# First FFN: meta products of gate and up in one group, a pair's differences put off, the first gate's sums in the opening

## The chip, the cores and the metric

The kernel runs on one core of a Trainium2 chip. Its engines are TensorE (PE, with the weight loads shown apart as PEld), VectorE (DVE), ScalarE (ACT), GpSimd (POOL) and SyncE (SP, whose queue issues most transfers); each works through its own instructions in order. The metric is the device time of one execution in microseconds.

## The reference

One layer of a hybrid decoder for 1024 tokens and 16 learned meta tokens, in float32, with model width 1024 and a feed-forward width of 2816:

```python
def swiglu(h, w_in, w_out):
    gu = h @ w_in
    g, u = jnp.split(gu, 2, axis=-1)
    return (jax.nn.silu(g) * u) @ w_out

# h = h + 1/2 * swiglu(rms_norm(h))         first feed-forward layer (FFN)
# u = rms_norm(h) @ w_in                    projection
# o = concat[hgrn2(u), stick_breaking(u)]   parallel heads
# h = h + o @ w_out
# h = h + 1/2 * swiglu(rms_norm(h))         second FFN
```

The change touches the first FFN, and in one place the second product of both FFNs.

## The kernel before

**Numbers in two halves.** A float32 operand is split into a high half in fp32r (a cast on ACT, L360, `wh`) and the rest (a subtraction on DVE, L362, `wl`). A product is the sum of high by high, low by high and high by low (`times`, L430). Four blocks of 128 in the contracted dimension make 12 matmuls of 128x128 by 128x512 for one product.

**Seven products for eight.** `fast_in` computes x @ w_in for a block of 256 columns of the weights, as a 2x2 of blocks by the 2x2 of the tokens and model halves, with seven products in place of eight. One such block is a quad. Its order on TensorE is: B11 (bank qa), T2 (qb), B21 (qa), T3 (qb), the meta tokens' small products, T1 (qc), T4 (qb), B22 (qc). Their weights are a11, s2, a12, s3, s1, a22 and s4 in this order: three raw blocks, and four sums made on POOL (L384): s1 = a21 + a22, s2 = s1 - a11, s3 = a11 - a21, s4 = a12 - s2. Between products DVE or ACT read the bank: `p1` after B11, u2 = p1 + qb after T2 (L462, `kept`), u3 after T3. T3 adds into the same bank as T2, so it may start only when DVE has read u2. In the same way B21 adds into qa after p1 was read. `take` reads the four output banks (L504 to L507 for the gate, L513 to L517 for the up quad).

**Pairs.** A gate quad and the up quad of the same 256 columns are a pair; there are 11 (f = 0, 2 ... 20). `up` multiplies silu(gate) by up into `sg`, and after the last of the four quarters `combined` makes four differences of them on DVE (L533 twice, L540, L543), which the second product needs as operands; POOL stores each of them (L529, L520). The first four pairs, the openers, run with gate and up in turns. Their first two products stand in the opening, in which tokens are transposed, scaled and halved into TensorE's operands (`open_tokens`; L829 to L831 for the differences that T2 and T3 are made of, L892 for T4's).

**Meta tokens.** The 16 meta tokens go through the same weights with 32-column matmuls (`meta_in`): `begin` does 16 of them per quad in the tile `mq` (32 records in the trace, four at a time on quarters of the array, L937); ACT copies the result (`mt`, L947), and `finish`, called by the next group, adds the pieces up with a matmul by `pick` (`mf`, L917) followed by Silu or the product with it. The meta group is the last reader of a quad's raw blocks, so the next quad's loads (L373, on SP) wait for it: `in_bufs` raw buffers, six.

**What sets the order.** TensorE's order in the first FFN is the order in which the code is written. In `open_tokens` that of ACT, DVE and SP is too. Elsewhere a scheduler orders ACT, DVE, POOL and SP; `issue_after` adds an edge to it. `between` (one step of a list of work for later stages at 54 `hooks`) splits the weights of the projection and the second FFN ahead of time: an early load on SP (L152), a cast on ACT (L174), a subtraction on DVE (L175) and a store on SP (L169), in `both` tiles.

**Second product.** `fast_out` multiplies the stored activations by w_out in the same way (products L685, weights and operands split in L617 and L618). It evicts a finished set of four banks into `hT` with four DVE operations (L657), for most steps delayed to the second quarter of the next step.

## Time and profile before

| What | us |
| --- | --- |
| median of three runs | 2023.78 |
| lowest and highest | 2022.3, 2026.27 |
| profiled execution, device time | 2020.56 |
| its span in the trace | 2018.8 |

The device time of the profiled execution is 1.8 us longer than its span. Times in the trace count from the span's start, and L12 is line 12 of the program. In the rows of a timeline stand start, duration, engine, line, operation, output and inputs by the program's names, the tile's shape and how many were put together; in brackets, how long the engine was idle ahead of it and what it waited for. In tables of waits stand the engine and line that waited, what they waited for, and then the total in us, how many times, and the longest. The stages of the span are: start to 16, opening to 100, opener pairs to 203, single pairs to 490, the first FFN's second product to about 700, then projection, mixing and the second FFN from 1380 to the end.

### The profile page before, as it was taken

The numbers are of one execution on the slowest core, as the hardware profiler recorded it, in microseconds if no ns is written. First come the engines' busy times: TensorE is split into PE (matmuls) and PEld (weight loads), VectorE is DVE, ScalarE is ACT, GpSimd is POOL, SyncE is SP. The second block draws the span as 40 slices with busy tenths as digits, with TensorE's granted clock in tenths as the row PEclk, the third lists the DMA queues.
The fourth block names the chain that finished last, engine by engine and source line by source line (L and its number), as shares of the span: only waits on it lengthen the run. The fifth ranks groups of instructions, "written<-read, shape, count | busy, mean of one in ns | idle before, by whom it ended". The sixth has DMA issues, their size and how long they took to land.

```text
span 2018.8 us, 30806 instructions
## 1 busy us (share of the span) xinstructions
PE 1964.1 (97%) x10940; PEld 1646.2 (82%) x10940; DVE 1356.4 (67%) x2052; ACT 860.8 (43%) x1742; POOL 583.5 (29%) x692
## 2 busy tenths in 40 slices
PE   7999999999999999999999999999999999999998
PEld 6788777777878888888888888777888888888887
DVE  7867667787578663237767667558566766767764
ACT  6423333333444544456666635434132333344443
POOL 3443233332000002334333341320444545530000
PEclk9999999999999999999999999999999999999999
DMA  6266787757985416343545166664533233369363
GB/s 206 83 171 182 227 260 245 241 185 255 327 278 164 131 53 204 123 169 101 139 133 139 55 229 179 167 238 162 194 102 110 101 103 103 106 253 310 116 198 136
DMA packets 315578, 347.19 MB, mean 172 GB/s; under 512 B 61520, under 2 KB 216656, under 8 KB 315424
## 3 DMA queue, kind: packets, MB, share of 16 engines
q1 hardware_dynamic: 297136, 292.18, 46.0%
q0 software_dynamic: 17248, 53.03, 7.5%
q8 instruction: 87, 1.43, 0.3%
q14 instruction: 67, 0.55, 0.1%
q10 hardware_dynamic: 1040, 0.00, 0.0%
HBM read 233.75 MB, written 111.38 MB: 171 GB/s over the span
## 4 chain that ended last, share of the span: by engine, by line
PE 82%; DVE 7%; DMA 5%; issue 3%; ACT 2%; POOL 1%; SPq 0%; DVEq 0%; POOLq 0%; ACTq 0%
PE o L685 18%; PE qb L430 16%; PE qc L430 11%; PE qa L430 10%; PE proj L249 5%; PE proj L251 5%; PE proj L250 5%; PE flip L1366 2%; DMA raw<-in_ffn_w_out_dram 1%; PE wo L250 1%; PE wo L249 1%; PE wo L251 1%; PE mq L937 1%; PE oacc L1436 1%; PE oacc L1438 1%
## 5 line engine op out<-in xcount | busy, mean ns | idle before, releaser
L430 PE MATMUL qb<-T,wh 128*128 128x512 f32 x1056 | 346.0, 391 | 10.1 <-DVE u L462 7.5
L430 PEld LDWEIGHTS qb<-T,wh 128*128 128x128 f32 x1056 | 198.1, 188 | 58.4 <-ACT both L174 5.7
L430 PE MATMUL qa<-B,wh 128*128 128x512 f32 x696 | 227.0, 390 | 2.2 <-DVE sum L513 1.9
L362 DVE TENSOR_TENSOR wl<-s,wh 128x512 fp32r<-128x512 f32 x160 | 183.4, 1147 | 60.4 <-ACT wh L360 59.3
L249 PE MATMUL proj<-xh,wh 128*128 128x512 f32 (+2 forms) x640 | 216.5, 338 | 0.8 <-DVE st L1059 0.7
L685 PE MATMUL o<-t,w 128*128 128x512 f32 x924 | 213.1, 391 | 1.3 <-DVE w L618 1.1
L251 PE MATMUL proj<-xl,wh 128*128 128x512 f32 (+2 forms) x640 | 209.7, 328 | 0.8 <-DVE xl L1821 0.8
L250 PE MATMUL proj<-xh,wl 128*128 128x512 f32 (+2 forms) x640 | 209.9, 328 | 0.0
L685 PE MATMUL o<-parts 128*128 128x512 f32 x924 | 209.9, 389 | 0.0
L430 PE MATMUL qb<-T,wl 128*128 128x512 f32 x528 | 206.0, 390 | 1.5 <-DVE wl L362 1.4
L685 PEld LDWEIGHTS o<-t,w 128*128 128x128 f32 x924 | 172.6, 188 | 39.0 <-DVE w L618 1.5
L685 PEld LDWEIGHTS o<-parts 128*128 128x128 f32 x924 | 173.4, 188 | 36.0
L360 ACT CAST wh<-s 128x512 fp32r<-128x512 f32 x160 | 99.4, 622 | 227.1 <-PE qb L430 168.3
L430 PEld LDWEIGHTS qa<-B,wh 128*128 128x128 f32 x696 | 130.5, 188 | 30.3 <-ACT T L309 2.3
L384 POOL TENSOR_TENSOR s<-raw 128x512 f32<-128x512 f32 x80 | 109.8, 1372 | 153.6 <-DMA raw<-in_ffn_w_in_dram 89.3
L430 PE MATMUL qa<-B,wl 128*128 128x512 f32 x348 | 135.5, 389 | 0.0
L360 ACT CAST wh<-raw 128x512 fp32r<-128x512 f32 x120 | 74.5, 621 | 142.6 <-PE qc L430 103.7
L251 PEld LDWEIGHTS proj<-xl,wh 128*128 128x128 f32 x640 | 120.5, 188 | 12.3 <-DVE xl L1821 1.2
L249 PEld LDWEIGHTS proj<-xh,wh 128*128 128x128 f32 x640 | 120.7, 189 | 11.4 <-DVE st L1059 1.2
L250 PEld LDWEIGHTS proj<-xh,wl 128*128 128x128 f32 x640 | 120.6, 188 | 9.1
L1518 POOL TENSOR_TENSOR sig<-sig,keep 128x144 f32<-128x144 f32 (+3 forms) x64 | 81.4, 1273 | 133.7 <-DVE keep L1512 94.1
L430 PE MATMUL qc<-T,wh 128*128 128x512 f32 x352 | 118.6, 398 | 0.0
(392 smaller groups left out, 4023.2 us busy)
## 6 DMA issues: line engine op xcount, KB each, us to landing
raw<-in_ffn_w_in_dram SPq DMA_DIRECT2D x176, 256.0 KB, 3.5
raw<-in_ffn_w_out_dram SPq DMA_DIRECT2D x121, 256.0 KB, 4.4
w2in<-both SPq DMA_DIRECT2D x28, 512.0 KB, 2.9
raw<-in_w_in_dram SPq DMA_DIRECT2D x25, 512.0 KB, 4.1
ks<-kD SPq DMA_DIRECT2D x32, 260.0 KB, 4.8
wout<-both SPq DMA_DIRECT2D x16, 512.0 KB, 3.8
wh<-w2in SPq DMA_DIRECT2D x27, 256.0 KB, 3.2
wl<-w2in SPq DMA_DIRECT2D x27, 256.0 KB, 3.2
```

The costliest lines, as they stand in the source:

```text
L249: nc.tensor.matmul(ps, wh[:, s], xs, start=k == 0, stop=False)
L250: nc.tensor.matmul(ps, wl[:, s], xs, start=False, stop=False)
L251: nc.tensor.matmul(ps, wh[:, s], xl[:, k, c0 : c0 + n], start=False, stop=k == nk - 1)
L360: nc.scalar.copy(hi, src)
L362: nc.vector.tensor_sub(lo, src, hi.bitcast(F32))
L384: taken(op(t, x, y), False)
L430: nc.tensor.matmul(ps, a[:, k, :], b[:, k, :], start=start and k == 0 and i == 0, stop=k == 3 and i == 2, skip_group_check=True,)
L685: nc.tensor.matmul(banks[bank][m], y[:, m * P : (m + 1) * P], z, start=start and at == 0 and e == 0, stop=q == nq - 1 and e == 2, skip_gro ...
L937: nc.tensor.matmul(ps[at : at + 32, :], self.xm[:, 4 * h + k, :], blocks[i, h][:, k, :], start=h == 0 and kk == 0, stop=h == 1 and kk == 1 ...
L1366: self.nc.tensor.transpose(ps[:m, j, :], src[:, s0 : s0 + m], self.ident)
L1436: nc.tensor.matmul(o[:, c], vj, w[0], start=j == 0, stop=False, skip_group_check=True)
L1518: nc.gpsimd.tensor_mul(sig, sig, keep[:, 1 : nk + 1])
```

## The change

Seven edits, by place:

- Meta products (`meta_in`): the gate's blocks are kept, and gate and up are multiplied in one group of 32 matmuls (64 records) in the up quad, ahead of its T1; one copy of `mt` and two `mf` matmuls in a row. There are 11 groups instead of 22. `in_bufs` goes from 6 to 10.
- `put_off`: `combined` of a pair in the first FFN is called in the next gate quad, after its u3, that is, after its T3 is written out.
- `prepare`: the first gate's four blocks are loaded and its four sums made on POOL at the opening's item 4. Their buffers and the early loads' are divided differently (early loads 8 to 4; raw blocks of the opening come from the common pool).
- The opening: T2's differences are made with T2's and T3's halves, those of T4 only behind the last tokens' work; T4's and B22's halves come a step later each.
- `split_ahead`: a plain group is one piece, and a load goes ahead only where both groups fit in four buffers. The list has 58 steps instead of 54 and still 54 hooks; what is left over is done at the start of the second product (three `both` copies).
- `fast_out`: a delayed eviction of four banks is done in two halves, two banks in the second quarter and two in the fourth.
- A filler tile is 32 instead of 288 columns.

```diff
-                t = self.early_raw.tile([P, 512], F32, tag="raw", name="early", bufs=8)
+                t = self.early_raw.tile([P, 512], F32, tag="raw", name="early", bufs=4)
...
-            nxt = load(groups[0][0])
-            yield None
-            for (_, makes), after in zip(groups, groups[1:] + [((), None)]):
-                raws, nxt = nxt, load(after[0])
+            ahead = []
+            for i, (views, makes) in enumerate(groups):
+                if not ahead:
+                    ahead.append(load(views))
+                    yield None
+                raws = ahead.pop(0)
+                after = groups[i + 1 : i + 2]
+                if after and len(views) + len(after[0][0]) <= 4:
+                    ahead.append(load(after[0][0]))
...
-        return [
-            ([v for _, v in pieces[i : i + 4]],
-             [(d, lambda raws, j=j: raws[j]) for j, (d, _) in enumerate(pieces[i : i + 4])])
-            for i in range(0, len(pieces), 4)
-        ]
+        return [([v], [(d, lambda raws: raws[0])]) for d, v in pieces]
...
-        loaded = []
-
-        def block(i, h, col, turns=0):
-            if turns == 2:
-                t = self.early_raw.tile([P, 4, P], F32, tag="raw", name="raw", bufs=self.ahead_bufs)
-            else:
-                t = wp.tile([P, 4, P], F32, tag="raw", name="raw", bufs=self.in_bufs)
...
+        prepared = {}
+        quarters = (0, 0), (1, 0), (1, 1), (0, 1)
+
+        def first_sums(blocks, turns):
+            a11, a21, a22, _ = blocks
+            s1 = made(a21, nc.gpsimd.tensor_add, a22, turns)
+            return s1, made(s1, nc.gpsimd.tensor_sub, a11, turns)
+
+        def prepare(col):
+            blocks = [block(i, h, col) for i, h in quarters]
+            a11, a21, _, a12 = blocks
+            s1, s2 = first_sums(blocks, 2)
+            s3 = made(a11, nc.gpsimd.tensor_sub, a21, 2)
+            prepared[col] = blocks, (s1, s2, s3, made(a12, nc.gpsimd.tensor_sub, s2, 2))
...
-            blocks = [block(i, h, col, turns) for i, h in quarters]
+            blocks, sums = prepared.pop(col, (None, None))
+            blocks = blocks or [block(i, h, col) for i, h in quarters]
             a11, a21, a22, a12 = blocks
             if not opened:
                 yield operand(a11)
-            s1 = made(a21, nc.gpsimd.tensor_add, a22, turns)
-            s2 = made(s1, nc.gpsimd.tensor_sub, a11, turns)
+            if sums:
+                s1, s2, s3, s4 = sums
+            else:
+                s1, s2 = first_sums(blocks, turns)
             yield operand(s2)
             if not opened:
                 yield operand(a12)
-            yield operand(made(a11, nc.gpsimd.tensor_sub, a21, turns))
+            yield operand(s3 if sums else made(a11, nc.gpsimd.tensor_sub, a21, turns))
             if meta:
-                meta(col, zip(quarters, blocks))
+                meta(col, [(q, b) for q, b in zip(quarters, blocks)])
             yield operand(s1)
             yield operand(a22)
-            yield operand(made(a12, nc.gpsimd.tensor_sub, s2, turns))
+            yield operand(s4 if sums else made(a12, nc.gpsimd.tensor_sub, s2, turns))
...
+            if put_off:
+                put_off.pop()()
...
+                elif meta:
+                    put_off.append(combined)
...
-        def evict(bank, i, j, step):
-            for m in range(4):
+        def evict(bank, i, j, step, ms=range(4)):
+            for m in ms:
                 h = hT[:, 4 * i + m, cs[j] : cs[j] + n]
                 nc.vector.scalar_tensor_tensor(
                     h, banks[bank][m], 0.5, h, ALU.mult, ALU.add
                 )
-            ready(step)
+            if 3 in ms:
+                ready(step)
...
-                if q == 1 and delayed:
-                    evict(*delayed.pop())
+                if q in (1, 3) and delayed:
+                    evict(*delayed[0], range(q - 1, q + 1))
+                    if q == 3:
+                        delayed.pop()
...
-            sub(t2[j], b22[j], b11[j])
...
+            sub(t2[j], b22[j], b11[j])
...
-            4: lambda: (self.row_sum(meta, 8, junk, nc.scalar), sums(3)),
+            4: lambda: (self.row_sum(meta, 8, junk, nc.scalar), sums(3), prepare(0)),
...
-            for j in range(4):
-                sub(b21[j], b21[j], t2[j])
+            with self.tc.issue_after(last[1].ins):
+                for j in range(4):
+                    sub(b21[j], b21[j], t2[j])
             pools["t2"].close()
             operands("T4")
+            yield
             for j in range(4):
                 self.halve(ops["T4"], b21[j], j)
-            yield
             pools["b21"].close()
             operands("B22")
+            yield
             for j in range(4):
                 self.halve(ops["B22"], b22[j], j)
...
         def finish():
-            col, t = waiting.pop()
-            ps = self.pin.tile([P, 2, META], F32, tag="qd", name="mf", bufs=2)
-            nc.tensor.matmul(ps, t, self.pick, start=True, stop=True)
+            f, t = waiting.pop()
+            ps = self.pin.tile([P, 2, 2, META], F32, tag="qd", name="mf", bufs=2)
+            for i in range(2):
+                nc.tensor.matmul(ps[:, i], t[:, i], self.pick, start=True, stop=True)
             with ExitStack() as c:
-                for ins in marks.values():
-                    c.enter_context(self.tc.issue_after(ins))
-                if col < D_FF:
-                    nc.scalar.activation(self.sgm, ps, AF.Silu)
-                else:
-                    f = (col - D_FF) // P
-                    nc.vector.tensor_mul(self.actm[:, f : f + 2, :META], ps, self.sgm)
+                after_marks(c)
+                nc.scalar.activation(self.sgm, ps[:, 0], AF.Silu)
+                nc.vector.tensor_mul(self.actm[:, f : f + 2, :META], ps[:, 1], self.sgm)
+
+        gates = {}
 
         def begin(col, blocks):
+            if col < D_FF:
+                gates[col] = blocks
+                return
             if waiting:
                 finish()
-            blocks = dict(blocks)
-            ps = self.pin.tile([P, P], F32, tag="qd", name="mq", bufs=2)
-            for h in range(2):
-                for kk in range(2):
-                    for i in range(2):
-                        for kp in range(2):
-                            k, at = 2 * kk + kp, 32 * (2 * i + kp)
-                            nc.tensor.matmul(
-                                ps[at : at + 32, :], self.xm[:, 4 * h + k, :],
-                                blocks[i, h][:, k, :], start=h == 0 and kk == 0,
-                                stop=h == 1 and kk == 1, tile_position=(0, at),
-                                skip_group_check=True,
-                            )
-            t = self.metas.tile([P, P], F32, tag="mt", name="mt", bufs=2)
+            ps = self.pin.tile([P, 2, P], F32, tag="qd", name="mq", bufs=2)
+            for at_g, got in enumerate((gates.pop(col - D_FF), blocks)):
+                got = dict(got)
+                for h in range(2):
+                    for kk in range(2):
+                        for i in range(2):
+                            for kp in range(2):
+                                k, at = 2 * kk + kp, 32 * (2 * i + kp)
+                                nc.tensor.matmul(
+                                    ps[at : at + 32, at_g, :], self.xm[:, 4 * h + k, :],
+                                    got[i, h][:, k, :], start=h == 0 and kk == 0,
+                                    stop=h == 1 and kk == 1, tile_position=(0, at),
+                                    skip_group_check=True,
+                                )
+            t = self.metas.tile([P, 2, P], F32, tag="mt", name="mt", bufs=2)
             with ExitStack() as c:
-                for ins in marks.values():
-                    c.enter_context(self.tc.issue_after(ins))
+                after_marks(c)
                 nc.scalar.copy(t, ps)
-            waiting.append((col, t))
+            waiting.append(((col - D_FF) // P, t))
...
-                self.metas.tile([P, 288], F32, name="even")
+                self.metas.tile([P, 32], F32, name="even")
...
-                    self.t_bufs, self.in_bufs, self.ahead_bufs = 2, 6, 8
+                    self.t_bufs, self.in_bufs = 2, 10
...
-                    first, hooks, steps_ahead = 32, 54, 54
+                    first, hooks, steps_ahead = 32, 54, 58
```

What happens on DVE where the opening reads bank qa of the second pair's up quad (L513 before, L530 after, `sum<-qa,sum`), in rows of DVE ahead of it. Tiles b and t are token blocks; L831 and L871 are T2's differences. Before:

```order
L892 TENSOR_TENSOR b_238<-b_238,t_245 128x512
L362 TENSOR_TENSOR wl<-raw,wh 128x512
L829 SCALAR_TENSOR_TENSOR b_250<-xps,g_74,b_250 128x512
L830 SCALAR_TENSOR_TENSOR t_254<-xps,ng_90,b_258 128x512
L831 TENSOR_TENSOR t_246<-b_258,b_250 128x512
L362 TENSOR_TENSOR wl<-raw,wh 128x512
L829 SCALAR_TENSOR_TENSOR b_251<-xps,g_74,b_251 128x512
L830 SCALAR_TENSOR_TENSOR t_255<-xps,ng_90,b_259 128x512
L831 TENSOR_TENSOR t_247<-b_259,b_251 128x512
L513 TENSOR_TENSOR sum<-qa,sum 128x512
```

After, with the rows that follow:

```order
L854 SCALAR_TENSOR_TENSOR t_253<-xps,ng_90,b_257 128x512
L363 TENSOR_TENSOR wl<-raw,wh 128x512
L853 SCALAR_TENSOR_TENSOR b_250<-xps,g_74,b_250 128x512
L854 SCALAR_TENSOR_TENSOR t_254<-xps,ng_90,b_258 128x512
L363 TENSOR_TENSOR wl<-raw,wh 128x512
L853 SCALAR_TENSOR_TENSOR b_251<-xps,g_74,b_251 128x512
L854 SCALAR_TENSOR_TENSOR t_255<-xps,ng_90,b_259 128x512
L530 TENSOR_TENSOR sum<-qa,sum 128x512
L363 TENSOR_TENSOR wl<-raw,wh 128x512
L871 TENSOR_TENSOR t_244<-b_256,b_248 128x512
L311 TENSOR_TENSOR T_765<-t_244,T_764 128x512
L311 TENSOR_TENSOR T_763<-t_252,T_762 128x512
```

The differences L831 and L892 stood ahead of the sum; now T2's (L871) stand behind it, each with the halves that need it, and those for T4 (L917) follow much later, behind the two u2.

DVE from the last sum of an up quad (`u<-qc`) to the u2 of the next gate quad (`u<-qb,p`), where the sixth pair follows the fifth; `t<-sg`, `t<-sg,t` and `sg` are the four differences of `combined`. Before:

```order
L516 TENSOR_TENSOR u<-qc,u_2769 128x512
L362 TENSOR_TENSOR wl<-raw,wh 128x512
L517 TENSOR_TENSOR sg<-u,sg 128x512
L175 TENSOR_TENSOR both<-early,both 128x512
L533 TENSOR_TENSOR t<-sg 128x512
L533 TENSOR_TENSOR t<-sg,t 128x512
L540 TENSOR_TENSOR sg<-sg 128x512
L543 TENSOR_TENSOR sg<-sg,t 128x512
L362 TENSOR_TENSOR wl<-s,wh 128x512
L462 TENSOR_TENSOR u_2983<-qb,p_2960 128x512
```

After, at the same place:

```order
L533 TENSOR_TENSOR u<-qc,u_2717 128x512
L363 TENSOR_TENSOR wl<-raw,wh 128x512
L534 TENSOR_TENSOR sg<-u,sg 128x512
L180 TENSOR_TENSOR both<-early,both 128x512
L552 TENSOR_TENSOR t<-sg 128x512
L552 TENSOR_TENSOR t<-sg,t 128x512
L559 TENSOR_TENSOR sg<-sg 128x512
L363 TENSOR_TENSOR wl<-s,wh 128x512
L562 TENSOR_TENSOR sg<-sg,t 128x512
L477 TENSOR_TENSOR u_2939<-qb,p_2916 128x512
```

The four differences stand ahead of u2 in both; one weight row moved between the third and the fourth. At the six boundaries of the single pairs there are 19, 19, 19, 19, 18 and 20 rows of DVE from the up quad's sum of T1 to this u2 before, and 18, 18, 19, 19, 19 and 19 after. In the opener pairs, two of the four differences come behind u2.

SP, where it loads the raw blocks of a later quad (`raw<-in_ffn_w_in_dram`) among early loads, token rows for the meta tokens' path and stores of `both`. Before:

```order
L373 DMA raw<-in_ffn_w_in_dram 128x4x128 x4
L964 DMA xrow<-in_x_dram 128x512
L152 DMA early<-in_w_out_dram 128x4x128
L169 DMA win_847<-both 256x1x512
L169 DMA win_848<-both 256x1x512
L152 DMA early<-in_w_out_dram 128x4x128
```

After:

```order
L152 DMA early<-in_w_out_dram 128x4x128
L371 DMA raw<-in_ffn_w_in_dram 128x4x128 x8
L174 DMA win_863<-both 256x1x512
L152 DMA early<-in_w_out_dram 128x4x128
L174 DMA win_864<-both 256x1x512
L152 DMA early<-in_w_out_dram 128x4x128
L174 DMA win_864<-both 256x1x512
L152 DMA early<-in_w_out_dram 128x4x128
L1018 DMA xD<-xts 32x16x32
L996 DMA xrow<-in_x_dram 128x512
L1018 DMA xD<-xts 32x16x32
```

Four loads for each quad were two bursts in a pair; now eight for a pair go out in one, and the other transfers stand together behind and ahead of it.

19 lines of the change are left out of this document (13 added, 6 removed).

## The prediction

> **What bounds the kernel now.** I read the page's table of engines and its chain of waits first, then the busy time of each engine by stage, then what TensorE (PE) waited for, and last the timelines around its longest waits.
>
> ```profile
> PE 1964.1 (97%) x10940; PEld 1646.2 (82%) x10940; DVE 1356.4 (67%) x2052; ACT 860.8 (43%) x1742; POOL 583.5 (29%) x692
> PE 82%; DVE 7%; DMA 5%; issue 3%; ACT 2%; POOL 1%; SPq 0%; DVEq 0%; POOLq 0%; ACTq 0%
> ```
>
> TensorE is busy for 97% of the span, and the chain that ended last runs through it for 82%. So a saving must be either work taken from PE or one of its waits. The second view gives the waits by stage: the stretch, its length, then busy time of PE, PEld, DVE, ACT and POOL, granted clock, DMA share and GB/s.
>
> ```profile
> 16.00:100.00 84.00, 80.48 (x424) 64.34 (x425) 72.69 (x111) 50.54 (x92) 25.32 (x21) 1.00 0.41 114
> 100.00:203.00 103.00, 102.86 (x623) 83.81 (x622) 73.13 (x103) 29.47 (x56) 42.47 (x45) 1.00 0.62 173
> 203.00:490.00 287.00, 277.47 (x1606) 226.82 (x1606) 213.16 (x297) 112.61 (x211) 98.56 (x95) 1.00 0.71 231
> 490.00:600.00 110.00, 108.73 (x550) 88.03 (x549) 77.16 (x126) 42.87 (x76) 5.43 (x10) 1.00 0.91 317
> PE qb L430 <- DVE u L462: 7.5, 5, 2.0
> PE qa L430 <- DVE sum L513: 1.9, 1, 1.9
> PE qb L430 <- DVE wl L362: 1.4, 3, 0.6
> PE qb L430 <- ACT both L174: 1.2, 1, 1.2
> PE qc L430 <- DVE wl L362: 0.8, 1, 0.8
> ```
>
> Length less PE's busy time leaves 3.5 us idle in the opening (16 to 100), 0.1 in the opener pairs, 9.5 in the single pairs (203 to 490) and 1.3 at the start of the second product. The rows below them (total us, times, longest) say what was late. In the single pairs five of six waits come where one pair ends and the next begins: T3 may not add into its bank before DVE has read u2 (L462) from it, 7.5 us. A sixth, 1.2 us, is put down to ACT. The granted clock is 1.00 in all four stretches, so none of this is throttling. What these places can give is at most some 15 us of idle, and the small matmuls of the meta tokens beside it.
>
> **Meta products in one group.** Here is one group as it runs now, with the load that it lets go, and how long its weight loads take.
>
> ```profile
> 266.07 0.39 PE L430 MATMUL qb<-T,wh 128*128 128x512 f32 x1
> 266.30 0.30 PE L917 MATMUL mf<-pick,mt 128*128 128x32 f32 x2
> 266.54 1.08 PE L937 MATMUL mq<-raw,xm 128*32 128x128 f32 x32
> 267.55 0.50 PE L430 MATMUL qc<-T,wh 128*128 128x512 f32 x1
> 267.88 0.39 PE L430 MATMUL qc<-T,wl 128*128 128x512 f32 x1
> L937 PEld LDWEIGHTS mq<-raw,xm x704: 106/110/110, 80.7 to 481.5; 128*32 128x32 f32 x176
> 267.24 2.29 SPq L373 DMA_DIRECT2D raw<-in_ffn_w_in_dram  x4
> ```
>
> Matmuls of a product follow one another at 0.23 us (266.07 to 266.30). From mf to the next product the group puts in 267.55 - 266.30 = 1.25 us, and the product's first step then takes 0.33 where 0.23 is usual, so 1.35 us in all, 22 times (704 records by 32). One group now does the work of two: the 32 records of the second quad run four abreast, so 8 steps of 0.110 = 0.88 us, and its second mf adds between 0.1 and 0.24 (the spacing of two mf records against the whole 266.30 to 266.54). A pair falls from 2.70 to between 2.33 and 2.47 us. That is 2.5 to 4.1 us over 11 pairs; I take **3.3**. A loss is excluded, since the operations are the same and one entry and one exit fall away per pair. Mt copies and Silus are fewer on ACT, which has time.
>
> **The opening.** PE is late four times; the largest is here, with DVE and POOL ahead of it.
>
> ```profile
> 57.53 0.39 PE L430 MATMUL qa<-B,wh 128*128 128x512 f32 x1
> 59.87 0.47 PE L430 MATMUL qa<-B,wh 128*128 128x512 f32 x1 [1.94 <-DVE sum L513]
> 50.35 1.71 DVE L831 TENSOR_TENSOR t<-b,b 128x512 f32<-128x512 f32 x1
> 52.09 1.67 DVE L892 TENSOR_TENSOR b<-b,t 128x512 f32<-128x512 f32 x1
> 55.60 0.68 DVE L831 TENSOR_TENSOR t<-b,b 128x512 f32<-128x512 f32 x1
> 58.12 0.99 DVE L831 TENSOR_TENSOR t<-b,b 128x512 f32<-128x512 f32 x1
> 59.04 0.68 DVE L513 TENSOR_TENSOR sum<-qa,sum 128x512 f32<-128x512 f32 x1
> 47.26 1.29 POOL L384 TENSOR_TENSOR s<-raw 128x512 f32<-128x512 f32 x1 [4.00 <-DMA raw<-in_ffn_w_in_dram]
> ```
>
> Before L513 may read bank a, DVE does the differences for T2 (L831) and two of B21 (L892). The change moves them behind it. The rows show 1.71 + 1.67 + 0.68 + 0.99 = 5.05 us taken out of the queue against a wait of 1.94, so this wait should go. Two of those rows are long because POOL adds at the same time; those adds now come at item 4, some 20 us earlier. Idle 3.5 plus a restart of about 0.2 each (the 0.33 against 0.23 above, and 57.53 to 59.87 is 2.34 where 0.23 + 1.94 would be 2.17) is 4.3 us. T2's differences now stand between T2's and T3's own halves, so the short waits for T3 and wl (1.4 and 0.8 above) may keep a part. Ends: 0.5 (only the rows themselves, and new waits for most of it) to 4.3; I take **3.3**, nearer the upper end because the move removes more than twice the wait. The four loads that come earlier run with a DMA share of 0.41, and the opening's POOL has 25 of 84 us busy, so they have room.
>
> **The boundaries.** This is the longest one: DVE and PE while the pair from 250 to 284 ends.
>
> ```profile
> 270.62 0.69 DVE L516 TENSOR_TENSOR u<-qc,u 128x512 f32<-128x512 f32 x1 [2.71 <-PE qc L430]
> 276.45 1.69 DVE L362 TENSOR_TENSOR wl<-s,wh 128x512 fp32r<-128x512 f32 x1 [2.42 <-ACT wh L360]
> 282.26 0.68 DVE L533 TENSOR_TENSOR t<-sg 128x512 f32<-128x512 f32 x1
> 284.19 0.69 DVE L543 TENSOR_TENSOR sg<-sg,t 128x512 f32<-128x512 f32 x1
> 285.39 0.68 DVE L462 TENSOR_TENSOR u<-qb,p 128x512 f32<-128x512 f32 x1
> 272.97 1.42 POOL L384 TENSOR_TENSOR s<-raw 128x512 f32<-128x512 f32 x1 [7.28 <-DMA raw<-in_ffn_w_in_dram]
> 286.22 0.47 PE L430 MATMUL qb<-T,wh 128*128 128x512 f32 x1 [2.05 <-DVE u L462]
> ```
>
> The causes stand one behind the other. The meta group frees the weight buffers, SP issues the next gate's loads at 267.24, POOL's first sum starts at 272.97, DVE gets its next operand at 276.45 after 2.42 us of idle, and from there it works without a break to u2 at 285.39. In that queue stand the four differences, 282.26 to 284.19 and 0.69 more: 2.6 us. If they really left it, the wait of 2.05 would be gone. But the emitted order after the change has them still ahead of u2 at each of the six single-pair boundaries (the rows are in the section on the change); TensorE's order alone is written by hand, DVE's is the scheduler's. From the up quad's sum of T1 (the row at 270.62) to u2 there stand 19, 19, 19, 19, 18, 20 rows before and 18, 18, 19, 19, 19, 19 after, so 2 fewer in six. So I cost the putting off itself at nothing at these places; among the opener pairs two of four do go behind u2, but PE idles only 0.1 us there.
>
> What does help is the group's length. The first load goes out 0.70 us after the group's start (266.54 to 267.24), and T3's turn comes a fixed number of products after its end. With 8 more steps of 0.110 behind the release, load, sum, operand and queue get 0.88 us more. With a third of a row of 0.6 less per boundary, that is about 1.07 us at each of six, whose idle is 7.5 + 1.2 = 8.7, 1.45 on average, with 0.2 more for the restart: 6.4 at most by this. DVE also loses time to POOL in an uneven way (1.69 for the subtraction at 276.45, 0.69 for the one at 284.19), and one boundary waits on ACT, so I take **5.3**. Ends: 0, where DVE works through a boundary without any idle and so gets no use of an earlier load, and 10 (all idle of 203 to 490 and its restarts).
>
> **The second product's start and its eviction.**
>
> ```profile
> 561.36 1.10 PE L685 MATMUL o<-t,w 128*128 128x512 f32 x2 [1.06 <-DVE w L618]
> 558.23 2.48 DVE L657 SCALAR_TENSOR_TENSOR hT<-o,hT 128x512 f32<-128x512 f32 x4
> 498.51 0.69 DVE L543 TENSOR_TENSOR sg<-sg,t 128x512 f32<-128x512 f32 x1 [3.73 <-DMA act110B<-sg]
> 499.73 0.50 PE L685 MATMUL o<-t,w 128*128 128x512 f32 x1
> ```
>
> Four evictions in a row hold DVE for 2.48 us, and PE then waits 1.06 for a w. Halves of 1.24, one two products later, leave room for that w: **0.8** gained, 0 to 1.3. On the other side, `both` copies that the hooks no longer reach are emptied at this start, and a w that stood ahead of the last difference now stands behind it. That difference waited 3.73 us for a store and ended at 499.20, and PE's next matmul of this product stands at 499.73, with little to spare. Three more rows and one late w at 0.7 to 0.8 us each: **1.2** lost, 0 to 3.
>
> **The loads.** SP now issues eight loads in one burst instead of four and four. Four take 2.29 us to issue; so the burst takes 4.6, and what stands behind it (a token row, the next early load, the store of `both`) is 2.3 us later. In the single pairs ACT waits for such stores already.
>
> ```profile
> ACT both L174 <- DMA wout<-both: 5.1, 3, 2.5
> ```
>
> ACT casts weights in its own order, so a `both` that waits for a free buffer holds the next wh. I take **0.6** lost, between 0 and 4 (seven pairs at the 0.6 that one more wait like these, 5.1 in three, would cost after the 1.1 us or so that a product leaves). The sum: -3.3 - 3.3 - 5.3 - 0.8 + 1.2 + 0.6 = -10.9. The profiled execution took 2020.56 us (span 2018.8), 3.2 below the median of the three runs, so it would become 2009.7; against the median 2023.78 it is 2012.9. I forecast **2013**, by itself between 2008 and 2018.
>
> **Rivals.** First, DVE is the bound at the boundaries, and 0.88 us later only moves the wait. For it: the queue from 276.45 to 285.39 has no break. Against it: the 2.42 ahead of it is idle. Then -3.3 - 3.3 - 0.8 + 1.8 = -5.6, **2018**.
>
> Second, the stalls go altogether, because the differences run late enough in practice or the longer group covers all of them: -3.3 - 4.3 - 10 - 1 = -18.6, **2005**. The 1.45 us on average against 1.07 speaks for it, the order of DVE against it.
>
> Third, on the other side: the burst of eight sits on SP ahead of the transfers that free `both`, ACT stops in its order, and the wait goes from DVE to ACT. A burst 2.3 us longer, not covered, at seven pairs is 16, against 10.9 gained: **2029**. It decides from 10.9 / 7 = 1.6 us a pair on. For it: ACT's waits on such stores reach 2.5 us now, and one boundary already ends on ACT. Against it: only three were seen, and the order spreads the early loads between the bursts.
>
> Fourth, POOL holds DVE in the opening. These rows are three sums of POOL, and DVE beside them.
>
> ```profile
> 314.28 1.28 POOL L384 TENSOR_TENSOR s<-raw 128x512 f32<-128x512 f32 x1 [5.17 <-DMA raw<-in_ffn_w_in_dram]
> 316.03 1.77 DVE L517 TENSOR_TENSOR sg<-u,sg 128x512 f32<-128x512 f32 x1
> ```
>
> An operation of two SBUF tiles takes 1.77 us where 284.19 shows 0.69, so each of the four prepared sums can cost DVE 1.1, some 4.3 in all, at a time when it scales the first tokens' operands for PE. If none of it is covered, the opening's 3.3 turns to +1 and the total is -6.6, **2017**. [...] Against it: PE in the opening waits for the tokens to come, and DVE has 11 of 84 us free.
>
> **How the numbers follow.** Forecast 0.55, boundaries unchanged 0.16, no stalls 0.10, burst 0.12, POOL in the opening 0.07. What a measurement of this kernel can tell from no change is about 0.2%, 4 us: faster is below 2019.7, slower above 2027.8. Nearly all of the forecast, all of the second and most of the first and fourth lie below: 0.54 + 0.10 + 0.10 + 0.05 = 0.79. Between: 0.01 + 0.06 + 0.02 and a third of the burst's (a part of its price), 0.13. Above: 0.08. The range from 2004 to 2022 leaves out most of the third and what lies beyond the second.
>
> **What would show it.** Eleven rows of mq groups with 64 records and 2.2 to 2.4 us from mf to the next product: the first term; more than 2.6 would refute it. No wait on L530 near 57 us, and under 1.5 us idle in the opening. At the boundaries `u` before `t` in few places, waits of qb on DVE's u below 4 us in total; if they stay at 7, the first rival holds. A wait of qb on ACT's `both` above 3 us is the third. At the second product's start one wait of 1 to 2 us and none near 561. A time above 2022 would mean that the burst or the start cost more than any row here shows.

## The result, and the profile after

The changed kernel takes 2027.58 us (median of 17 runs), the kernel before 2023.78 in as many. The ratio is 1.0017, with a 95% interval from 1.0008 to 1.0026: slower by 3.4 us, with 1.6 and 5.3 as the ends. The forecast was 2013, so it was wrong, and in its sign too. The profiled execution has a span of 2023.6 us against 2018.8.

First the busy time by stage of the changed kernel (length, then PE, PEld, DVE, ACT, POOL, granted clock, DMA share, GB/s), and PE's waits on u2 up to 600 us (total, times, longest).

```profile
16.00:100.00 84.00, 78.80 (x417) 62.91 (x418) 71.77 (x109) 49.23 (x89) 24.74 (x20) 1.00 0.42 115
100.00:203.00 103.00, 102.49 (x627) 84.50 (x626) 78.92 (x106) 30.33 (x55) 47.06 (x49) 1.00 0.63 175
203.00:490.00 287.00, 276.24 (x1598) 227.41 (x1597) 213.15 (x290) 111.89 (x202) 96.76 (x93) 0.99 0.70 223
490.00:600.00 110.00, 105.93 (x532) 84.25 (x531) 79.04 (x130) 41.64 (x75) 5.43 (x10) 1.00 0.95 326
PE qb L445 <- DVE u L477: 11.8, 8, 2.4
```

PE's idle time went from 3.5 to 5.2 us in the opening, from 9.5 to 10.8 in the single pairs and from 1.3 to 4.1 at the second product's start; the opener pairs add 0.4. That is 6.1 us more. The waits on u2, which the change was aimed at, rose from 7.5 us (five times) to 11.8 (eight times, two of them in the opening and the openers). The granted clock, 1.00 before, is 0.99 in the single pairs, and that too is time: here are one boundary's last wait and the two stretches behind it.

```profile
328.06 0.47 PE L445 MATMUL qb<-T,wh 128*128 128x512 f32 x1 [2.37 <-DVE u L477]
328.00:331.00 3.00, 2.94 (x8) 2.34 (x9) 2.63 (x2) 0.00 (x0) 2.29 (x3) 0.57 1.13 328
331.00:334.00 3.00, 3.00 (x13) 2.43 (x12) 1.33 (x3) 0.62 (x1) 0.77 (x1) 0.87 0.46 128
```

In 3 us stand 8 matmuls where the usual 0.23 us each make 13. About 3.4 us run at half clock and cost some 1.6; it happens at two boundaries. Against this stands the meta group, whose size is as forecast:

```profile
265.19 0.53 PE L948 MATMUL mf<-pick,mt 128*128 128x32 f32 x4
265.64 1.95 PE L970 MATMUL mq<-raw,xm 128*32 128x128 f32 x64
267.53 0.50 PE L445 MATMUL qc<-T,wh 128*128 128x512 f32 x1
```

From mf to the next product it takes 2.34 us; with the 0.10 of a slow first step that is 2.44 against 2 x 1.35, or 0.26 saved in each of 11 pairs, 2.9 us. Idle 6.1, clock 3.2 and group -2.9 make 6.4. The projection's first matmul, which follows the first FFN, stands 6.6 us later than before (723.20 against 716.64), so the stages account for the first FFN. The spans differ by 4.8: 0.4 us are won back between there and the last matmul, and 1.4 behind it; why was not followed up.

**The opening.** The wait for which the differences were moved is gone: L530 runs at 55.94, where L513 stood at 59.04. But PE now waits three times later on (DVE first, then PE).

```profile
55.94 0.68 DVE L530 TENSOR_TENSOR sum<-qa,sum 128x512 f32<-128x512 f32 x1
74.01 1.28 DVE L477 TENSOR_TENSOR u<-qb,p 128x512 f32<-128x512 f32 x2
75.21 2.49 DVE L917 TENSOR_TENSOR b<-b,t 128x512 f32<-128x512 f32 x4
77.82 0.69 DVE L477 TENSOR_TENSOR u<-qb,p 128x512 f32<-128x512 f32 x1
74.75 0.50 PE L445 MATMUL qb<-T,wh 128*128 128x512 f32 x1 [1.22 <-DVE u L477]
79.16 0.50 PE L445 MATMUL qb<-T,wl 128*128 128x512 f32 x1 [1.16 <-DVE wl L363]
83.27 0.50 PE L445 MATMUL qc<-T,wl 128*128 128x512 f32 x1 [1.08 <-DVE wl L363]
```

The four differences for T4 stand for 2.49 us between two u2, and the weights wl come late behind them.

**A boundary.** The queue of DVE from the up quad's T1 to u2, its first and last rows, and what POOL does at its end:

```profile
312.13 0.69 DVE L533 TENSOR_TENSOR u<-qc,u 128x512 f32<-128x512 f32 x1 [3.70 <-PE qc L445]
...
325.56 1.75 DVE L562 TENSOR_TENSOR sg<-sg,t 128x512 f32<-128x512 f32 x1
327.24 0.68 DVE L477 TENSOR_TENSOR u<-qb,p 128x512 f32<-128x512 f32 x1
```

```profile
325.29 1.47 POOL L382 TENSOR_TENSOR s<-raw,s 128x512 f32<-128x512 f32 x1
```

DVE had been waiting 3.70 us for PE when T1 ended, and then worked 15.8 us without a break (312.13 to 327.92), against the 13.6 that PE needs for the five products up to T3. The last difference takes 1.75 us, where 0.69 is usual, while POOL makes the next gate's fourth sum beside it. It is not the only long row: three near the queue's start take 1.5 to 1.8 us beside POOL's first three sums (one of them is shown with e12 below), as they did in the kernel before (1.77 at 316.03 in the prediction's rows).

**The second product's start.** Leftover stores on SP, the next loads there, and who waited for them on ACT and PE:

```profile
492.59 0.32 SPq L174 DMA_DIRECT2D w2in<-both  x1
495.59 1.52 SPq L174 DMA_DIRECT2D w2in<-both  x2
510.26 1.58 SPq L624 DMA_DIRECT2D raw<-in_ffn_w_out_dram  x3
515.32 0.62 ACT L638 CAST w<-raw 128x512 fp32r<-128x512 f32 x1 [9.35 <-DMA raw<-in_ffn_w_out_dram]
515.99 0.49 PE L707 MATMUL o<-t,w 128*128 128x512 f32 x1 [1.30 <-ACT w L638]
```

The same three loads of w_out in the kernel before:

```profile
503.49 2.06 SPq L603 DMA_DIRECT2D raw<-in_ffn_w_out_dram  x3
```

The product's first matmul, before and after:

```profile
490.57 1.62 PE L685 MATMUL o<-t,w 128*128 128x512 f32 x6
493.31 0.93 PE L707 MATMUL o<-t,w 128*128 128x512 f32 x3 [0.49 <-DVE u L533]
```

The loads go out 6.8 us later. The whole product starts 2.7 us later, so 4.0 us are lost within it, behind three stores of 512 KB that were not there; ACT has nothing to cast for 9.35 us.

### The profile page after: what moved, and what is told of

It is laid out like the page before. It is cut to its first block, busy times and chain, and to the rows that moved or that the text cites. A ratio compares the mean times of both kernels' runs of the same rounds, so it can differ in the third digit from the quotient of the medians.

```text
span 2023.6 us, 30784 instructions
## 1 busy us (share of the span) xinstructions
PE 1964.1 (97%) x10940; PEld 1647.1 (81%) x10940; DVE 1365.5 (67%) x2052; ACT 861.0 (43%) x1731; POOL 584.2 (29%) x692
## 4 chain that ended last, share of the span: by engine, by line
PE 76%; DVE 4%; DMA 3%; issue 2%; ACT 1%; POOL 0%; SPq 0%; DVEq 0%; POOLq 0%; ACTq 0%
PE o L707 18%; PE qb L445 13%; PE qc L445 9%; PE qa L445 8%; PE proj L250 5%; PE proj L252 5%; PE proj L251 5%; PE flip L1398 2%; DMA raw<-in_ffn_w_out_dram 1%; PE wo L250 1%; PE wo L251 1%; PE wo L252 1%; PE lvl L1191 1%; PE oacc L1468 1%; PE oacc L1470 1%
## 5 line engine op out<-in xcount | busy, mean ns | idle before, releaser
L445 PE MATMUL qb<-T,wh 128*128 128x512 f32 x1056 | 348.2, 394 | 13.8 <-DVE u L477 11.8
L363 DVE TENSOR_TENSOR wl<-s,wh 128x512 fp32r<-128x512 f32 x160 | 184.2, 1151 | 57.1 <-ACT wh L361 55.8
L252 PEld LDWEIGHTS proj<-xl,wh 128*128 128x128 f32 x640 | 120.5, 188 | 12.2 <-DVE xl L1853 1.2
L445 PEld LDWEIGHTS qb<-T,wl 128*128 128x128 f32 x528 | 99.9, 189 | 21.7 <-DVE wl L363 1.6
```

Of the source, the lines that this page charges most:

```text
L252: nc.tensor.matmul(ps, wh[:, s], xl[:, k, c0 : c0 + n], start=False, stop=k == nk - 1)
L363: nc.vector.tensor_sub(lo, src, hi.bitcast(F32))
L445: nc.tensor.matmul(ps, a[:, k, :], b[:, k, :], start=start and k == 0 and i == 0, stop=k == 3 and i == 2, skip_group_check=True,)
```

## The experiments

All ratios are to the kernel before, run beside each kernel on the same chip. The changed kernel's is 1.0017; differences between two ratios are uncertain by some 0.13 to 0.18%, 2.6 to 3.7 us. A trace is of one execution, which can lie some us off its kernel's median: those of e4 and e6 took 2018.78 and 2007.46 us, 6 us less.

**Putting the differences off, undone (e1).** The call stands at the pair's end again:

```diff
-                elif meta:
-                    put_off.append(combined)
                 else:
                     combined()
```

> The changed kernel, but a pair's four differences are called at the pair's own end, as before. First theory (the scheduler puts them ahead of u2 in either case, so putting them off did nothing): within 2 us of the changed kernel's 2027.6, and the waits of qb on DVE's u in the single pairs stay at 10 to 13 us. Rival (putting off is what delays u2): 3 us or more below the changed kernel, with these waits back at 7 to 8 us.

2022.09 us, ratio 0.9996 (0.9987 to 1.0005). That is 0.21% below the changed kernel, the rival's side. At each boundary the order of DVE differs in a single row, a weight row. The change put it between the third and the fourth difference at the first two boundaries, and between the second and the third at the other four; here it stands behind the fourth again. The next rows are DVE and POOL at the boundary near 414 in this kernel.

```profile
412.65 0.68 DVE L560 TENSOR_TENSOR sg<-sg,t 128x512 f32<-128x512 f32 x1
413.85 0.68 DVE L477 TENSOR_TENSOR u<-qb,p 128x512 f32<-128x512 f32 x1
414.18 1.29 POOL L382 TENSOR_TENSOR s<-raw,s 128x512 f32<-128x512 f32 x1
414.68 0.47 PE L445 MATMUL qb<-T,wh 128*128 128x512 f32 x1 [1.36 <-DVE u L477]
```

The weight row frees the buffer of POOL's fourth sum. Behind the last difference, the sum falls beside u2, which reads a bank and takes its 0.68; ahead of the third, the sum falls beside the fourth difference, which then takes 1.75. So what was costed at nothing costs 1.1 us at the four later boundaries of the changed kernel, and there the waits reach 1.8 to 2.4 us, and at two of them the granted clock is 0.50 for 3.4 us. The wait here is 1.36, and the clock stays at 1.00. Putting off also has a gain, which this run gives up: in the opener pairs PE is idle for 2.7 us here and for 0.5 in the changed kernel.

**The differences really behind u2 (e2).** An edge forces the order that the change names:

```diff
             if put_off:
-                put_off.pop()()
+                with self.tc.issue_after(adds[-2]):
+                    put_off.pop()()
```

(`adds` holds the additions of u2 and u3.)

> The changed kernel, with an edge that makes the scheduler put the four differences behind the next gate's u2. First theory (DVE's queue from the up quad's T1 to u2 is the bound at the boundaries, 15.8 us against five products of 13.6): 2.6 us leave the queue, the waits of qb on DVE's u in the single pairs fall from 11.8 to under 4 us, no stretch with a lower granted clock is left there, and the time is 7 to 13 us below the changed kernel, 2015 to 2021. Rival (the burst of eight loads or POOL's sums set the boundary): within 2 us of the changed kernel.

2013.01 us, 0.9949 (0.9937 to 0.9962), 2 us better than the range expected. PE's waits on u2 in the single pairs, with this kernel's busy times there:

```profile
PE qb L445 <- DVE u L477: 2.0, 4, 0.9
203.00:490.00 287.00, 283.78 (x1648) 234.18 (x1646) 229.72 (x312) 115.97 (x210) 101.86 (x103) 1.00 0.75 241
```

The queue that took 15.8 us takes 11.6 to 12.2 here. DVE's queue to u2 sets the boundaries, and the four differences were the piece to take from it. One wait of 2.2 us on a w now stands in the second product, and the granted clock from 490 to 600 is 0.98 instead of 1.00.

**The weight copies early (e3).** Two steps at four of the hooks, so that none is left over:

```diff
-                        if i > 0 and steps_ahead * i // hooks > steps_ahead * (i - 1) // hooks:
+                        if i > 0:
...
-                                next(turning[1], None)
+                                for _ in range(steps_ahead * i // hooks - steps_ahead * (i - 1) // hooks):
+                                    next(turning[1], None)
```

> The changed kernel, with two steps at some hooks, so that no weight copies are left for the start of the second product. First theory (the three copies and their stores of 512 KB on SP are what the stretch from 480 to 600 us lost): 3 to 5 us below the changed kernel, 2022.5 to 2024.5, and the waits at the second product's start sum to under 2 us where they were 4. Rival (the split eviction or the eight loads in a burst cost that time): within 1.5 us of the changed kernel, the waits near 516 and 568 stay.

2013.26 us, 0.9954 (0.9941 to 0.9966): ten us better than expected. The stretch from 490 to 600 of this kernel, and its waits on u2 in the single pairs:

```profile
490.00:600.00 110.00, 109.82 (x554) 88.98 (x553) 75.60 (x122) 44.91 (x80) 3.79 (x7) 1.00 0.90 311
PE qb L445 <- DVE u L477: 4.5, 4, 2.4
```

Idle at the second product falls from 4.1 to 0.2 us, about what was expected. The rest came at the boundaries, which the theory had not counted: moved by a few hooks, a copy or its sum fewer, or both, stand in DVE's queue at the last four of them (17 rows from the T1 sum to u2 at the last three, instead of 19, and 18 instead of 19 at the one ahead of them). The second boundary has one row more, 19 for 18, and the wait of 2.4 stands there. One or two DVE rows of 0.6 decide at these places.

**The opening's differences back (e4).** The subtractions for T2 and T4 and the two `yield`s in their old places, the sums still early:

```diff
             stt(t3[j], ps, self.ng1[:, j : j + 1], b22[j], ALU.mult, ALU.add)
+            sub(t2[j], b22[j], b11[j])
...
-            sub(t2[j], b22[j], b11[j])
             self.halve(ops["T2"], t2[j], j)
...
-            with self.tc.issue_after(last[1].ins):
-                for j in range(4):
-                    sub(b21[j], b21[j], t2[j])
+            for j in range(4):
+                sub(b21[j], b21[j], t2[j])
```

> The changed kernel, with the differences for T2 and T4 and T4's and B22's halves of the opening back in their old places; the first gate's sums still made early on POOL. First theory (the differences were moved from a stretch in which DVE has idle time into one in which it has none): TensorE's idle time from 16 to 100 us falls from 5.2 to between 2 and 3.5 us, the time is 1.5 to 3 us below the changed kernel. Rival (the early sums on POOL are what costs the opening): idle stays at 4.5 to 5.5 us or more, the time within 1 us.

2025.1 us, 1.0006 (0.9997 to 1.0016). The time alone hardly parts it from the changed kernel (0.11% below), but the stage does:

```profile
16.00:100.00 84.00, 80.74 (x431) 65.20 (x431) 74.31 (x113) 50.60 (x91) 26.15 (x21) 1.00 0.42 117
```

PE is idle for 3.3 us instead of 5.2. The move took DVE work from the stretch up to 56 us, where DVE has gaps, into the one up to 84, where it has hardly any: from 16 to 56 us DVE is idle for 7.6 us in the changed kernel and 4.5 here, from 56 to 84 for 1.5 and 1.7, and in the kernel before for none there.

**The first gate's sums late (e5).** `prepare(0)` taken out of the opening's item 4.

> The changed kernel, with the first gate's four sums made where they were before (the blocks loaded and summed with the first quad's weights) and the opening's differences in their new places. Theory (the early sums block DVE while it reduces the first rows, the moved differences are the larger loss): the wait of 0.6 near 32 us goes and DVE's row reductions near 25 and 29 us take 1.2 instead of 2.3, but the waits on u2 and wl from 74 to 83 us stay; 0 to 1.5 us below the changed kernel. Rival (without the early sums the weights of the first T2 come late): a new wait on POOL or wl between 55 and 75 us, 1 us or more above the changed kernel.

2025.51 us, 1.0013 (1.0003 to 1.0022): by time no more than the uncertainty below the changed kernel. One row reduction of DVE in the changed kernel, and then the same one here:

```profile
24.85 2.31 DVE L736 SCALAR_TENSOR_TENSOR junk<-row 128x1024 uint8<-128x1024 f32 x1
```

```profile
25.11 1.22 DVE L736 SCALAR_TENSOR_TENSOR junk<-row 128x1024 uint8<-128x1024 f32 x1
```

The sums cost DVE 1.1 us on each of two such rows, and PE 0.6 near 32 us. The waits from 74 to 83 stay, 1.22, 1.16 and 1.08 us as above, and no new one appears between.

**The meta products apart again (e6).** `meta_in` with the functions of before: 16 matmuls per quad, `mf` and `mt` for each; ten buffers.

> The changed kernel with the meta products again in a group of 16 per quad, buffers and all else as changed. Theory (the group saves 0.27 us of TensorE per pair and nothing at the boundaries, whose DVE queue starts only when the up quad's T1 has ended): 2 to 4 us above the changed kernel, the idle time of DVE ahead of the up quad's T1 sum falls from 3.7 to 2.7 us, the waits of qb on DVE's u stay within 2 us of 11.8. Rival (my forecast: the longer group gives the boundaries 0.88 us each): these waits grow by 4 us or more and the time by 7 or more.

2013.25 us, 0.995 (0.9935 to 0.9966). Both theories were wrong: it is 14 us faster than the changed kernel, with the group's 2.9 us given up. Its busy times in the single pairs:

```profile
203.00:490.00 287.00, 286.29 (x1667) 235.38 (x1657) 213.17 (x313) 118.13 (x217) 97.05 (x99) 1.00 0.74 239
```

Idle there is 0.7 us, with no wait on u2 at all. POOL's waits in the single pairs show what changed; first the changed kernel, then this one:

```profile
POOL s L382 <- DVE wl L363: 83.5, 14, 10.5
POOL s L382 <- DMA raw<-in_ffn_w_in_dram: 28.4, 4, 7.9
```

```profile
POOL s L382 <- DVE wl L363: 94.5, 19, 11.9
```

POOL no longer waits for a load. It makes a quad's first two sums right behind the last one of the quad before, ahead of need, and not beside the first rows of DVE's queue at the boundary. The queue takes 11.7 to 13.3 us instead of 14.0 to 15.8, less than PE's 13.6. The boundaries are not all of the 14 us: this kernel also loses less in the opening (3.5 us idle instead of 5.2) and at the second product's start (0.2 instead of 4.1).

**Seven buffers instead of ten (e9)**, meta products apart: `in_bufs` 7.

> The kernel with the meta products apart (e6_meta_apart, 2013.3) with seven raw buffers instead of ten. Theory now (ten buffers let a quad's loads and POOL's sums run a quad ahead, so that they no longer fall beside DVE's queue between the up quad's T1 and u2; the group of both quads holds eight of the ten and takes that away): with seven, waits of qb on DVE's u of 6 to 12 us come back at the single pairs, and the time is 2020 to 2027. Rival (it is the entry into the group, one long stretch of small matmuls, that disturbs the boundary): stays at 2010 to 2015, waits under 2 us.

2014.19 us, 0.9955 (0.9943 to 0.9968), and 0.7 us idle in the single pairs. The theory fell as it was put: seven do as well as ten. The sum s1 needs a21 and a22, the second and the third block. With six buffers and four held by a quad until its meta products, two blocks are loaded ahead, and a22 waits for the group. With seven it is three. With ten, of which a group of both quads holds eight, it is two again. (The kernel before has six, and POOL waits 55.8 us for loads in its single pairs; no run took six with the rest as here.)

**Eleven buffers with the group (e12).** The space comes from one of two `u` tiles:

```diff
-                    self.t_bufs, self.in_bufs = 2, 10
+                    self.t_bufs, self.in_bufs = 2, 11
```

> The changed kernel, meta products in one group, with eleven raw buffers instead of ten (the space from one of two u tiles). Theory now (POOL's first sum needs the third block of the next gate; six buffers less four held, and ten less the eight that the group holds, both leave two ahead, seven less four leave three): with three ahead the next gate's first sums no longer wait for a load, POOL's wait on raw in the single pairs (55.8 us before) falls below 20, the waits of qb on DVE's u fall from 11.8 to under 4 us, and the time to 2010 to 2017. Rival (the group itself disturbs the boundary, by its length): the waits stay at 9 us or more and the time within 3 us of the changed kernel's 2027.6.

2012.01 us, 0.9945 (0.993 to 0.996). POOL and PE in the single pairs:

```profile
POOL s L382 <- DVE wl L363: 95.8, 20, 10.5
PE qb L445 <- DVE u L477: 1.1, 1, 1.1
```

What that does to DVE's queue is seen in one of its rows, in the changed kernel with POOL's first two sums, the first of which had waited for a load, and then in this one:

```profile
312.48 1.29 POOL L382 TENSOR_TENSOR s<-raw 128x512 f32<-128x512 f32 x1 [6.13 <-DMA raw<-in_ffn_w_in_dram]
313.85 1.61 POOL L382 TENSOR_TENSOR s<-s,raw 128x512 f32<-128x512 f32 x1
314.24 1.77 DVE L534 TENSOR_TENSOR sg<-u,sg 128x512 f32<-128x512 f32 x1
```

```profile
313.27 0.69 DVE L534 TENSOR_TENSOR sg<-u,sg 128x512 f32<-128x512 f32 x1
```

In the changed kernel POOL's sums wait for a load and fall beside DVE's rows, which take 1.77 instead of 0.69; here they are done by then, and the queue takes 13.1 to 13.3 us at every boundary. The last difference is still long (1.78 at this place), but no wait comes of it. POOL's wait on loads is gone with the group kept. So it was the third block ahead, and not the group as such; one buffer is worth 0.7% of the time. Two things are left open: the run has one `u` tile instead of two, whose own effect was not separated, and PE still waits 2.5 us there for the last sums of the last pair (L533, 481 to 484 us).

**Evictions in one piece (e7)**, with the copies early: `evict` of four banks at the second quarter.

> The kernel with the copies early (e3_copies_early, 2013.3), and the four evictions in one piece again. Theory (the split eviction is worth the wait of 1.1 us near 561 of the kernel before): that wait of o on DVE's w comes back, 0.8 to 1.3 us, and the time is 0.5 to 2 us above e3. Rival (the split is worth nothing where no stores are in the way): no wait above 0.5 us between 500 and 600, time within 0.5 us.

2017.25 us, 0.9967 (0.9956 to 0.9978). The ratios of e3 and this one were taken on different chips and differ by 0.13%, within their uncertainty. The trace is clearer; PE, and then the stretch behind it:

```profile
559.82 6.37 PE L707 MATMUL o<-t,w 128*128 128x512 f32 x18 [1.65 <-DVE w L639]
560.00:565.00 5.00, 4.89 (x14) 3.65 (x15) 5.00 (x9) 1.14 (x2) 0.00 (x0) 0.67 0.98 368
```

The wait returns, larger than the 1.06 of before, and the granted clock behind it is 0.67 over 5 us. The split is worth its wait, some 1 us and more where the clock follows; that rests on this one wait of one trace, and e2 shows that a longer one can stand there with the split too.

**Together.** Differences forced late, copies early, opening back (e8):

> Three repairs together: differences behind u2, copies early, the opening's differences back. If their gains add (boundaries 11, start of the second product 5, opening 3, of which the first two overlap at the boundaries): 2006 to 2010, TensorE's idle time from 16 to 600 us under 8 us. If the boundaries have another limit right behind: 2010 to 2014.

2011.65 us, 0.9943 (0.993 to 0.9955). The gains did not add: at the boundaries the first two take rows from the same queue, and one wait of 2.24 us on a wl appears at 410 us. Next, meta products apart, copies early, opening back (e10):

> Meta products apart with ten buffers, copies early, the opening's differences back; the differences of a pair stay put off, as changed. Theory (the three act at different places; the boundaries have nothing left to gain): 3 to 5 us below e6, 2008 to 2011, TensorE idle under 4 us from 16 to 600. Rival (a DMA limit takes over): 2012 to 2015 as e6.

2007.54 us, 0.9929 (0.9915 to 0.9943), with these idle times in the opening, the single pairs and the second product's start: 2.0, 0.1 and 0.1 us.

```profile
16.00:100.00 84.00, 81.96 (x437) 65.87 (x436) 75.12 (x113) 51.67 (x95) 26.29 (x22) 1.00 0.42 118
203.00:490.00 287.00, 286.89 (x1649) 236.61 (x1648) 213.49 (x311) 118.30 (x216) 95.11 (x99) 1.00 0.76 246
490.00:600.00 110.00, 109.88 (x536) 89.54 (x536) 75.65 (x122) 45.05 (x80) 2.16 (x4) 1.00 0.87 296
```

The same with a pair's differences at the pair's own end (e11):

> As e10_apart_copies_back, but with a pair's differences at the pair's own end. Theory (with no waits left at the boundaries it does not matter where the last difference stands against a weight row): within 1.5 us of e10. Rival (putting off costs a contended operation in every pair, hidden or not): 2 us or more below e10.

2007.03 us, 0.9924 (0.9912 to 0.9937): the same within the uncertainty, so where no wait is left the last difference's place does not matter. And the group with eleven buffers, with the same two repairs (e13):

> As e12, with the copies early and the opening's differences back, beside e10 with the meta products apart. Theory (with three blocks ahead the group's own 0.27 us a pair are left as its gain): 1 to 4 us below e10's 2007.5. Rival (up's and gate's loads in one burst still cost more than that): at or above e10.

2009.01 us, 0.993 (0.9916 to 0.9943). Its ratio is that of e10, so the group's 2.9 us, which lie within the uncertainty, do not show as a gain. Kernels e10 and e11 are the fastest, by 0.7% against the kernel before and 0.9% against the changed one.

## Why the prediction was wrong

**Meta group:** right in size, 0.26 us a pair against the 0.3 that 3.3 over 11 pairs makes. What failed is beside it: that a loss is excluded. The operations cost less, but the blocks that they hold kept the third load of the next gate waiting, with four buffers more than before. Against the kernel before this is a gain not taken and not a new loss: POOL's wait for these loads in the single pairs was 55.8 us before and 28.4 after.

**Boundaries:** forecast 5.3 us gained, measured 1.2 more idle and 3.2 at half clock, for which the sum had no term. The step that failed is "load, sum, operand and queue get 0.88 us more". It was drawn from one boundary at which DVE had been idle in mid-queue. The group stands ahead of T1, and the queue to u2 starts when T1 ends: the longer group made DVE's wait ahead of the queue longer (2.71 to 3.70) and left queue and products as they were. The first rival had this mechanism right, and its 2018 is still 10 us off. The third rival's 2029 came nearest to the time by luck, since its cause did not show (see the burst below); its sum also counts the burst's 0.6 twice. At the first two boundaries, one of which the step was drawn from, the wait did fall (1.47 to 0.58 and 2.05 to 0.72); at the other four it rose.

**Putting off:** rightly seen in the order that the four differences stay ahead of u2, and that they were the ones to move. Costed at nothing, though, and the one row that the order did show as moved was not followed to POOL. The order had been shown for the first boundary alone, where the move does no harm; it costs about 1.1 us at the four later ones (e1), while the edit as named is worth 0.47%, some ten us (e2 against e1).

**Opening:** forecast 3.3 gained, measured 1.7 more idle. The wait named did go. The step that failed is that work taken from ahead of a wait is a gain: 5 us of it were put where DVE had hardly any idle time, and the forecast's "may keep a part" stood for the whole of it. Not all of that is the differences: the fourth rival's price, 1.1 us an operation, was right, but only 0.6 us of it reached PE (e5). (Its 1.77 at 316.03 stands beside the second of POOL's three sums, at 315.64; the row that it shows is the first.)

**Second product's start:** a loss of the right kind and mis-sized: 1.2 forecast. Idle from 490 to 600 is 2.8 us more than before, and 3.9 more than with the copies early. The price was worked out from DVE's rows, and where PE waited was behind late loads of w_out. The stores on SP are a part of that and not all: e6 and e9 have the same three stores at this start, their loads go out 15.5 and 15.2 us after the product's first matmul, where it is 12.9 before and 17.0 in the changed kernel, and PE waits at most 0.3 us there. So the product can spare the stores' some 2.5 us; what adds the last 1.4 stays open. The split eviction was worth what was forecast (e7), but a late load hid it: in the changed kernel DVE waits 2.29 us for a load at 564.02, and PE 1.39 us at 567.90.

**Burst of eight loads:** PE's wait on ACT's `both` (1.2 us before) is gone from the single pairs, and none on ACT is longer than 0.7; this rival has no support. No run put the loads back into two bursts with the rest unchanged.

**The chances:** faster had 0.79. The terms were not independent, because several of them pressed on one queue, DVE's.

## What to carry to other kernels

Before a saving on the bottleneck engine is booked, follow what the longer-held buffers let start later: count the blocks ahead of need, not the buffers. Where one in-order queue sets a stall, take its start from the event that releases its first row, and let no row of it be costed at nothing until what POOL does beside it has been looked at. Work moved out of a queue is a gain only where the stretch that receives it has idle time.

## What the runs showed of the hardware

In the changed kernel a wait of TensorE of 2.37 us (up to 328.06) and one of 2.19 (up to 458.29) each went with 3.4 us at half clock (spacing 0.43 instead of 0.23, granted 0.57 in the rows at 328), and so did one of 1.65 us in e7 (granted 0.67 from 560 to 565). At waits of 2.20 us (415.28 in the changed kernel) and 1.65 (414.16 in the kernel before) the granted clock was 1.00, so the length of the wait alone does not decide. By the clock record of the changed kernel's trace the two slow stretches start at 328.39 and 458.10 us, the first 0.33 us behind the end of its wait and the second 0.19 ahead of it, and last 3.413 us each; their starts are 129.71 us apart, which is 38 times 3.413. What sets their start was not shown. At the spacings above, 3.413 us hold 8 matmuls instead of 15, so such a stretch cost an estimated 1.6 us on top of its wait.

An operation of VectorE with two tiles in SBUF took 1.75 to 1.79 us beside a sum of GpSimd (325.56 and 314.24 in the changed kernel, 401.62 in e6) and 0.68 to 0.69 without one (318.83 and 323.75 in the changed kernel), and a row reduction 2.31 instead of 1.22 (24.85 in the changed kernel, 25.11 in e5). An addition that reads a bank kept its 0.68 beside such a sum (284.04 and 404.24 in the changed kernel, 413.85 in e1).
